# A fourth pair of token tiles in the seven-product scheme of the v stage, and six products of later pairs made in the head

## The chip, the cores and the metric

The kernel runs on one core of a Trainium2 chip. The metric is the device time of one execution in microseconds; lower is better. A matmul runs on TensorE (PE), which accumulates into PSUM banks of 128x512 float32. ScalarE (ACT) and VectorE (DVE) move and combine data, GpSimd (POOL) issues the transfers that add into their destination, SyncE (SP) issues most of the others.

## The reference

One block on x of 1024 tokens by 1024 channels, all float32. Cut to what matters:

```python
h = rmsnorm(x, norm_g)
proj = h @ w_in                                   # 1024 x 7424
q, k, v, za, u, vs, zs, gm = split(proj)          # vs, u: 1024 columns each; k, v: 128 each
...                                               # attention branch a
sgo = chunked_spatial_gating(gelu(u), gelu(vs), sg_w, sg_b, sg_ln_g, sg_ln_b)
sgo = (sgo * silu(zs)) @ w_sg_out
ga, gs = split(sigmoid(gm + b_merge))
x = x + (ga * a + gs * sgo) @ w_o
out = rmsnorm(x, final_g)
```

`chunked_spatial_gating` applies a layernorm to gelu(vs) along the channels and mixes it within blocks of 128 positions, so gelu(vs) is needed with the tokens on partitions. Every other projection is made with its output channels on partitions.

## The kernel before

**Products.** A float32 operand is split into a high part (rounded to the matmul's format, a cast on ACT) and a low part (the rest, a subtraction on DVE); a product of two such operands takes three matmuls: high by high, high by low, low by high. A block product is 128 output rows by 512 columns over 512 of k: four steps of k by three, 12 matmuls, in one PSUM bank.

**The seven-product scheme.** A pair of 128-row tiles of one operand against 1024 columns over 1024 of k would be eight block products. The kernel makes seven, with sums and differences of the quarters of the other operand. Those forms are called b11, t1, t2, b21, t3, b22 and t4 (`FORMS`); each is held as a high and a low array of 128x4x512 (`new_b`). In the stages after the head the normalized input is the side with forms, made once, and the weights come in pairs of tiles ("pairs", `gemm_pair`), numbered n = 0, 1, ...: four of u (n = 0 to 3), one of key and value (4), four of q (5 to 8), and so on. Pair n takes seven parts of its weights: parts 0 and 1 are the two halves of the first raw tile, 2 to 5 come from two tiles of sums, 6 is half of the second raw tile. Products run in the order b11 (part 0), t1 (2), t2 (3), b21 (1), t3 (4), b22 (5), t4 (6). `split_next` makes the high and low arrays of the next parts in tiles `wh` and `wl`, of which there are three each; `pair_job` loads the raw tiles (`wr`, three in all) and `sums` makes the two tiles `s`.

**The head (the v stage).** The eight token tiles of x are loaded (`load_x`, into `wr`), scaled, transposed on TensorE (`scaled_part`) and moved out of PSUM into the float32 quarters f11, f21 (tiles 0 to 3) and f12, f22 (tiles 4 to 7); `cast_part` makes b11, b21 and b22 from the same banks. Here the tokens are the stationary side, and token tile p is paired with tile p + 4. `vs_gemm(t)` multiplies tile t by the first 512 columns of the vs weights: 8 steps of k, 24 matmuls; for tiles 1 to 3 in two banks of four steps, one to go on being accumulated into by the scheme. Before the change the pairs are (1, 5), (2, 6) and (3, 7). Tiles 0 and 4 are done in full: tile 0 in `first_tiles`, tile 4 by `vs_gemm(4)`, and the second 512 columns of both by `plain(c)`, c = 0 to 3. `take(name, c)` makes half of a form's products (two of the four steps of k) for every pair; the five forms are t1, t2, t3, b22 and t4. Weights of the forms are sums of chunks of the vs weights: `chain` (two tiles `s`) and `apart`, into which POOL adds chunk after chunk (`add_to`), and `ask`, a raw tile with or without one addition.

**Order.** Where the code stands under `tc.manual_schedule`, PE, ACT and DVE run in the order in which it is written; elsewhere a planner orders each engine's work by its own estimates of cost, and it always orders SP and POOL. `after` adds an order between two instructions, `paced` makes a transfer wait for a given instruction; `part_of_early` issues one of the transfers that sum later weights in DRAM (`sums`), paced by matmuls.

**After the head** come the statistics of tiles whose gelu is complete, `normalize`, and `mix`, issued from `hook` inside the u pairs.

Of the kernel before, what the change touches and what calls it, by code (L numbers as in the profile page):

```python
# [25 lines left out]
F32 = mybir.dt.float32  # L26
# [6 lines left out]
P = 128  # L33
D = 1024
# [20 lines left out]
def hybrid_tile(  # L55
# [92 lines left out]
    y_dr = scratch("y_dr")  # L148

# [152 lines left out]

    def make_sums(first=None, most=2):

        for _ in range(min(most, len(sums_to_make))):
            sums_to_make.pop(0)(first)

    def pair_job(n, load):


        def job():
# [109 lines left out]
    def gemm_pair(b, finish, hook=lambda: None, second="o", begun=None, last_form=None):  # L421
# [24 lines left out]
        t2 = bank(second)[:]  # L446
        product(t2, ready[n, 1], b["b21"], True)
# [185 lines left out]
    b12 = [mtile([P, 4, P], F32R, "x", 5)[:] for _ in range(2)]  # L633
# [54 lines left out]
    def normed_tile(t, scale=None):  # L688
        xt, r = scale or scale_of(t)
        if t == 4:  # L690
            hb.update(new_b(("b22",)))
            f.update((n, slot(at, dt=F32)) for n, at in (("f12", "t4h"), ("f22", "t3h")))
        for j in range(2):
            p3, copy, _, _ = scaled_part(t, j, xt, r)
            if t <= 4 or j:
                cast_part(t, j, p3)
            nc.scalar.copy(*copy)
# [34 lines left out]
    def vs_gemm(t, middle=None):  # L732

        acc = vs_acc[t] = bank("o" if t in (2, 3) else "mm")[:]
# [4 lines left out]
        for k in range(KC):  # L739
            if middle and k in middle:  # L740
                middle[k]()
            if t < 4 and k == 4:
                nc.scalar.copy(dst, acc)
                part = vs_acc["p1"]
            pace[0] = vs_step(part, t, k, *vs_w[k], (0, KC - 1) if t == 4 else (k & 4, k | 3))
        if t == 4:
            nc.scalar.copy(dst, acc)
        else:
            nc.vector.tensor_add(dst, dst, part)
# [13 lines left out]
    def first_tiles():  # L763
# [24 lines left out]
        acc0 = bank("mm")  # L788
        n_first = [0]

        def first_steps(k, *kinds):
            hi, lo = (v[:, k % 4, :] for v in quarter_of(0, k // 4))
            wh, wl = vs_w[k]
            for kind in kinds:
                lt, rt = {"hh": (hi, wh), "lh": (lo, wh), "hl": (hi, wl)}[kind]
                mm = nc.tensor.matmul(acc0[:], lt, rt, start=n_first[0] == 0, stop=n_first[0] == 3 * KC - 1)
                n_first[0] += 1
# [31 lines left out]
        nc.scalar.copy(xh[:, 0, 0:HALF], acc0[:])  # L829
# [31 lines left out]

    first_tiles()
    marks = []
    for t in range(5):
        if t == 4:
            vs_gemm(t, {2: lambda: marks.append(pace[0])})
        elif t > 1:
            vs_gemm(t)
        if t + 3 < NT:
            normed_tile(t + 3)  # L870
        if t == 3:
            x_in[7] = load_x(7)
        if t == 2:
            for c in range(2):
                chain.append(mtile([P, D], F32, "s", 2))
                copy_to(chain[c][:], w[W_VS + 4 + c])
        if t == 3:
            for c in range(2):
                of_chain(c)
            ask(6)  # L880
        if t == 4:
            for c in range(2):
                paced(add_to(chain[c][:], w[W_VS + 6 + c]), marks[0])
            copy_to(apart[:], w[W_VS + 4])
            add_to(apart[:], w[W_VS + 6])
            add_to(apart[:], w[W_VS])
            ask(7)
            of_raw()
# [5 lines left out]
    BY_SUMS = (0, 4, 5, 6, 7)  # L894
# [32 lines left out]
    t5s = {1: bank("tp")[:], 2: bank("tp")[:], 3: vs_acc[4]}  # L927

    def plain(c):
        wh, wl = weights[c]  # L930
        for t in (0, 4):
            for k in range(2):
                pace[0] = vs_step(others[t], t, 2 * c + k, wh[:, half_of(k)], wl[:, half_of(k)])
            if c == 3:
                gelu_of(t, 1, others[t])
# [3 lines left out]
    def take(name, c, done=None):  # L939
# [39 lines left out]
    others = {t: bank("sc")[:] for t in (0, 4)}  # L979
    def first_form(t):  # L980
        part = f11[:, :, tokens(t)]
        nc.vector.tensor_sub(part, part, f12[:, :, tokens(t)])

    for t in (4, 5, 6):
        first_form(t)
    with tc.manual_schedule(engines={mybir.EngineType.PE, mybir.EngineType.Activation, mybir.EngineType.DVE}):
        hb.update(new_b(("t1",)))
        first_form(7)
        form("t1", f11, (0,))
        plain(0)  # L990
        of_raw()
# [9 lines left out]
        for c in range(2):  # L1001
            ask(c, 4 + c)
# [153 lines left out]
    late.extend(lambda t=t: statistics_of(t) for t in (1, 2, 3))  # L1156
# [1191 lines left out]
```

## Time and profile before

| | |
|---|---|
| median of 3 runs | 894.8 us (894.44 to 895.01) |
| the profiled execution | 893.94 us |
| its span in the trace | 892.1 us |
| PE busy | 883.2 us, 4143 matmuls |
| DVE, ACT, POOL busy | 702.0, 560.5, 164.1 us |
| mean DMA rate | 239 GB/s |
| first matmul of form t1 of the v stage | 55.7 us |
| first matmul of u pair 0 | 96.5 us |

The page of the profile gives the busy time of each engine and the chain of work that ended last, followed back from the last instruction. Its groups and the answers of the trace name an instruction by line, engine, operation and output<-inputs (buffer numbers left out). Times are from the start of the span. Matmuls are pipelined, so a matmul that lasts 0.39 us in a row may start 0.23 us after the one before it; what counts is start to start.

### The profile page before, as it was taken

How to read it: one execution, taken by the hardware profiler on the slowest of the kernel's cores; microseconds unless marked ns; L12 is line 12 of the kernel's file. 1: busy time of each engine (PE TensorE's matmuls, PEld its weight loads, DVE VectorE, ACT ScalarE, POOL GpSimd, SP SyncE). 2: the span in 40 equal slices, each digit the busy share in tenths (PEclk: the TensorE clock that was granted, in tenths of full speed). 3: DMA queues.
4: the chain of work that ended last, by engine and by line, in shares of the span. 5: the costliest groups of instructions: out<-in, count | busy, mean ns of one | idle time of the engine just before them, and what ended most of it. 6: DMA issues, size and time to landing. Idle time of an engine off the chain costs nothing.

```text
span 892.1 us, 13277 instructions
## 1 busy us (share of the span) xinstructions
PE 883.2 (99%) x4143; PEld 732.8 (82%) x4143; DVE 702.0 (79%) x1358; ACT 560.5 (63%) x1096; POOL 164.1 (18%) x267
## 2 busy tenths in 40 slices
PE   8999999999999999999999999999999999999997
PEld 5888888888888888888888888888888888888886
DVE  7978866676688779888889887665798699579986
ACT  7877833333444568889888896443575385467444
POOL 3112122214021012323222100122201111110013
PEclk9999999999999999999999999999999999999999
DMA  8687588879788889999999993889869557988533
GB/s 291 162 216 191 171 167 177 179 208 265 256 269 266 277 238 247 285 302 283 284 343 291 280 258 116 302 318 251 228 190 345 198 198 262 293 253 274 193 112 125
DMA packets 131541, 213.32 MB, mean 239 GB/s; under 512 B 13100, under 2 KB 60848, under 8 KB 131472
## 3 DMA queue, kind: packets, MB, share of 16 engines
q1 hardware_dynamic: 108648, 148.83, 51.2%
q0 software_dynamic: 22672, 63.45, 30.1%
q8 instruction: 33, 0.54, 0.3%
q14 instruction: 36, 0.29, 0.1%
q10 hardware_dynamic: 152, 0.20, 0.1%
HBM read 155.68 MB, written 90.31 MB: 276 GB/s over the span
## 4 chain that ended last, share of the span: by engine, by line
PE 98%; DMA 1%; DVE 0%; SPq 0%; issue 0%; DVEq 0%; ACT 0%; ACTq 0%
PE ps_mm L399 45%; PE ps_o L399 27%; PE ps_tp L399 4%; PE ps_mm L701 2%; PE ps_two L1502 2%; PE ps_o L701 2%; PE ps_sc L399 2%; PE ps_sc L701 2%; PE ps_tp L1132 2%; PE ps_o L1639 2%; PE ps_tp L1577 2%; PE ps_tp L701 1%; PE ps_o L1647 1%; DMA wr<-in_x_dram 1%; PE ps_tp L1589 1%; PE ps_tp L678 1%
## 5 line engine op out<-in xcount | busy, mean ns | idle before, releaser
L189 DVE TENSOR_TENSOR wl<-wr,wh 128x512 fp32r<-128x512 f32 (+1 forms) x65 | 61.7, 951 | 71.6 <-ACT wh L188 71.4
L188 ACT CAST wh<-s 128x1024 fp32r<-128x1024 f32 (+1 forms) x68 | 67.8, 1000 | 73.4 <-issue 22.1
L188 ACT CAST wh<-wr 128x512 fp32r<-128x512 f32 (+1 forms) x65 | 54.0, 832 | 65.2 <-PE ps_mm L399 35.4
L189 DVE TENSOR_TENSOR wl<-s,wh 128x1024 fp32r<-128x1024 f32 (+1 forms) x68 | 79.2, 1164 | 8.8 <-ACT wh L188 8.4
L351 POOL DMA_DIRECT2D sums<-in_w_dram x48 | 35.3, 742 | 183.9 <-PE ps_mm L399 86.9
L399 PE MATMUL ps_o<-T_t1h,wh 128*128 128x512 f32 x148 | 58.4, 395 | 0.0
L399 PE MATMUL ps_o<-T_b22h,wh 128*128 128x512 f32 x148 | 57.9, 391 | 0.0
L399 PE MATMUL ps_o<-T_t1h,wl 128*128 128x512 f32 x148 | 57.8, 391 | 0.0
L399 PE MATMUL ps_o<-T_b22h,wl 128*128 128x512 f32 x148 | 57.8, 390 | 0.0
L399 PE MATMUL ps_o<-T_b22l,wh 128*128 128x512 f32 x148 | 57.8, 390 | 0.0
L399 PE MATMUL ps_o<-T_t1l,wh 128*128 128x512 f32 x148 | 57.7, 390 | 0.0
L1549 ACT ACTIVATE pr<-pr,sm 128x193 f32<-128x193 f32 (+2 forms) x128 | 56.0, 440 | 1.7 <-DVE sm L1533 1.0
L399 PE MATMUL ps_mm<-T_t4h,wh 128*128 128x512 f32 (+1 forms) x144 | 56.4, 392 | 0.0
L399 PE MATMUL ps_mm<-T_t3h,wh 128*128 128x512 f32 x140 | 55.5, 396 | 0.0
L399 PE MATMUL ps_mm<-T_t4h,wl 128*128 128x512 f32 (+1 forms) x144 | 55.4, 385 | 0.0
L399 PE MATMUL ps_mm<-T_t4l,wh 128*128 128x512 f32 (+1 forms) x144 | 55.4, 385 | 0.0
L399 PE MATMUL ps_mm<-T_b11h,wh 128*128 128x512 f32 x140 | 54.8, 392 | 0.0
L399 PE MATMUL ps_mm<-T_t3h,wl 128*128 128x512 f32 x140 | 54.7, 391 | 0.0
L399 PE MATMUL ps_mm<-T_b11l,wh 128*128 128x512 f32 x140 | 54.7, 390 | 0.0
L399 PE MATMUL ps_mm<-T_t3l,wh 128*128 128x512 f32 x140 | 54.6, 390 | 0.0
L399 PE MATMUL ps_mm<-T_b11h,wl 128*128 128x512 f32 x140 | 54.6, 390 | 0.0
L399 PE MATMUL ps_mm<-T_t2h,wl 128*128 128x512 f32 x140 | 54.6, 390 | 0.0
(500 smaller groups left out, 2531.8 us busy)
## 6 DMA issues: line engine op xcount, KB each, us to landing
wr<-in_w_dram SPq DMA_DIRECT2D x80, 256.0 KB
sums<-in_w_dram POOLq DMA_DIRECT2D x24, 512.0 KB, 6.6
s<-sums SPq DMA_DIRECT2D x24, 512.0 KB
wr<-in_w_dram SPq DMA_DIRECT2D x17, 512.0 KB
q_hl<-qhl SPq DMA_DIRECT2D x16, 512.0 KB
q<-q_hl SPq DMA_DIRECT2D x64, 128.0 KB
y_dr<-x POOLq DMA_DIRECT2D x28, 256.0 KB, 6.5
s_dr<-x SPq DMA_DIRECT2D x24, 256.0 KB
```

The source lines that it names most:

```text
L188: hi_casts.append(nc.scalar.copy(hi, src))
L189: return nc.vector.tensor_sub(lo, src, hi.bitcast(F32))
L351: return lambda: paced(nc.gpsimd.dma_start(dst, src, accum_op=op))
L399: mm = nc.tensor.matmul(acc, lt, rt, start=fresh and k == 0 and n == 0, stop=k == 3 and n == 2, skip_group_check=True,)
L678: turn = nc.tensor.transpose(pt[:, i * P : (i + 1) * P], xt[:, k * P : (k + 1) * P], ident[:])
L701: mm = nc.tensor.matmul(acc, lt, rt, start=first and n == 0, stop=last and n == 2, skip_group_check=True)
L1132: nc.tensor.matmul(pm[:, t * P : (t + 1) * P], xh[:, half * 4 + t, g * P : (g + 1) * P], bias[-1][1][:, g % 2, :], start=True, stop=True,)
L1502: nc.tensor.matmul(st.sc[:, i], q_of[:, c, i * P : (i + 1) * P], kt[:, :, lo:hi], start=True, stop=True)
L1549: nc.scalar.activation(v, v, AF.Exp, bias=st.nmax[:, c, i : i + 1], scale=-1.0, accum_out=st.sums[:, c, i : i + 1])
L1577: nc.tensor.transpose(st.inner[0 : P if st.t else 64, at : at + P], st.pr[:, i, place_of(c, 64 if st.t else P, 192)], ident[:],)
L1589: nc.tensor.transpose(st.ends[0:wide, i * P : (i + 1) * P], st.pr[:, i, 129 : 129 + wide], ident[:])
L1639: nc.tensor.matmul(st.po[:], lt, rt, start=i == 0, stop=False, skip_group_check=True)
```

## The change

Pair (0, 4) joins the scheme: `take` runs over p = 2, 3, 0, 1, tile 0 keeps its two halves of k in two banks, and `plain` and `vs_gemm(4)` go. Between the transposes of tiles 4 to 7 and form t1 stand instead six block products: the b21 product of pairs n = 0 to 5, whose form b21 is complete once tile 3 is transposed. Their weights (part 1 of each pair) are loaded into the unused second half of `xh` (`ask_ahead`), split in twos (`ahead_weights`), multiplied (`make_ahead`), copied by ACT and stored in DRAM (`copy_ahead`, tile `made_dr`). In `gemm_pair` pairs 0 to 5 read that product back: `split_next` splits only part 0 and loads the made product into the other half of the `wh` tile, and the x11 addition takes it from there in place of a PSUM bank. The transposes of tiles 4 to 7, the product of tile 3 and the six products stand in an order written out by hand. The chain additions of chunks 6 and 7 are issued with the chain's copies, no longer paced. Cut to its core:

```diff
+    made_dr = scratch("made_dr", (6, P, HALF))
...   # split_next
+        n = keys[0][0]
+        if keys == [(n, 0)] and n in IN_HEAD:
+            ready[n, 1] = hi[:, HALF:D].bitcast(F32)
+            copy_to(ready[n, 1], made_dr[n])
...
+    IN_HEAD = range(6)
...   # pair_job
+            first = (r0[:, 0:HALF], [(n, 0)]) if n in IN_HEAD else (r0[:], [(n, 0), (n, 1)])
...   # gemm_pair
-        t2 = bank(second)[:]
-        product(t2, ready[n, 1], b["b21"], True)
+        if n in IN_HEAD:
+            t2 = ready[n, 1]
+        else:
+            t2 = bank(second)[:]
+            product(t2, ready[n, 1], b["b21"], True)
         term[0] = nc.vector.tensor_add(x11[:], x11[:], t2)
...   # the head
+    def ask_ahead(n):
+        loads_of[n](xh[:, n, HALF:D], 0, 1)
+
+    def ahead_weights():
+        n = 2 * len(split_ahead)
+        parts = []
+        for tag in ("wh", "wl"):
+            parts.append(mtile([P, D], F32R, tag, 3))
+        split(*(v[:].rearrange("p (c n) -> p c n", c=2) for v in parts), xh[:, n : n + 2, HALF:D])
+        split_ahead.append(parts)
+
+    def make_ahead():
+        n = len(to_copy)
+        acc = vs_acc["p0" if n % 2 == 0 else "p1"]
+        product(acc, [v[:, half_of(n % 2)] for v in split_ahead[n // 2]], hb["b21"], True)
+        to_copy.append(acc)
+
+    def copy_ahead(n):
+        v = xtile()
+        pace[0] = nc.scalar.copy(v[:], to_copy[n])
+        copy_to(made_dr[n], v[:])
...
+    x_in[3] = load_x(3)
+    for n in (0, 1):
+        ask_ahead(n)
+    x_in[4] = load_x(4)
+    for n in range(2, 6):
+        ask_ahead(n)
+    normed_tile(3)
...
+    vs_gemm(2)
+    ahead_weights()
+    for c in range(2):
+        chain.append(mtile([P, D], F32, "s", 2))
+        copy_to(chain[c][:], w[W_VS + 4 + c])
+        add_to(chain[c][:], w[W_VS + 6 + c])
+    copy_to(apart[:], w[W_VS + 4])
+    add_to(apart[:], w[W_VS + 6])
+    add_to(apart[:], w[W_VS])
...
+    with ORDERED:
...
+        scale_both(4)
+        scales[5] = scale_of(5)
+        add_third = vs_gemm(3, {4: lambda: turn(4)}, True)
+        move_out(4)
+        scale_both(5)
+        ahead_weights()
+        scales[6] = scale_of(6)
+        add_third()
+        x_in[7] = load_x(7)
+        make_ahead()
+        turn(5)
+        scale_both(6)
+        scales[7] = scale_of(7)
+        make_ahead()
+        ask(0, 4)
+        copy_ahead(0)
+        move_out(5)
+        turn(6)
+        scale_both(7)
+        first_form(4)
+        ahead_weights()
+        make_ahead()
+        move_out(6)
+        copy_ahead(1)
+        ask(1, 5)
+        turn(7)
+        first_form(5)
+        first_form(6)
+        make_ahead()
+        move_out(7)
+        copy_ahead(2)
+        first_form(7)
...   # take
-        for p in (1, 2, 3):
+        for p in (2, 3, 0, 1):
...   # the five forms
         form("t1", f11, (0,))
-        plain(0)
-        of_raw()
+        of_chain(0)
+        make_ahead()
+        copy_ahead(3)
         form("t1", f11, (1,))
-        plain(1)
-        of_chain(0)
-        gelu_of(0, 0)
-        plain(2)
         of_chain(1, 1)
-        gelu_of(1, 0, n=3)
-        gelu_of(4, 0)
-        plain(3)
+        make_ahead()
+        copy_ahead(4)
+        copy_ahead(5)
+        for t in (0, 2):
+            gelu_of(t, 0, n=2)
```

`turn(t)` is the eight transposes of a tile, `scale_both(t)` its two scalings on DVE, `move_out(t)` its three moves on ACT and one low part on DVE, `first_form(t)` the subtraction f11 - f12 for its tokens.

More of the change, by code (lines that the diff above doesn't have):

```diff
@@ L308, in pair_job @@
     def pair_job(n, load):
+        loads_of.append(load)
         def job():
@@ L730, in hybrid_tile, with vs_gemm @@
     vs_acc = {}
-    def vs_gemm(t, middle=None):
-        acc = vs_acc[t] = bank("o" if t in (2, 3) else "mm")[:]
+    def vs_gemm(t, middle=None, later=False):
+        acc = vs_acc[t] = bank("sc" if t == 1 else "o")[:]
         part = acc
@@ L741, in vs_gemm @@
                 middle[k]()
-            if t < 4 and k == 4:
+            if k == 4:
                 nc.scalar.copy(dst, acc)
                 part = vs_acc["p1"]
[L745 to L749, printed above, removed]
+            pace[0] = vs_step(part, t, k, *vs_w[k], (k & 4, k | 3))
+        add = lambda: nc.vector.tensor_add(dst, dst, part)
+        return add if later else add()
     def in_order(*steps):
@@ L786, in first_tiles @@
         act = in_order(act, wide)
-        acc0 = bank("mm")
-        n_first = [0]
+        halves = [bank("mm")[:] for _ in range(2)]
+        vs_acc[0], vs_acc["p0"] = halves
+        n_first = [0, 0]
         def first_steps(k, *kinds):
@@ L795, in first_steps @@
                 lt, rt = {"hh": (hi, wh), "lh": (lo, wh), "hl": (hi, wl)}[kind]
-                mm = nc.tensor.matmul(acc0[:], lt, rt, start=n_first[0] == 0, stop=n_first[0] == 3 * KC - 1)
-                n_first[0] += 1
+                e = k // 4
+                mm = nc.tensor.matmul(
+                    halves[e], lt, rt, start=n_first[e] == 0, stop=n_first[e] == 11, skip_group_check=True
+                )
+                n_first[e] += 1
                 after(mm, turns[-1])
@@ L828, in first_tiles @@
         vs_gemm(1, {4: lambda: both(3, "hl"), 5: lambda: normed_tile(2, third)})
-        nc.scalar.copy(xh[:, 0, 0:HALF], acc0[:])
+        nc.scalar.copy(xh[:, 0, 0:HALF], halves[0])
+        nc.vector.tensor_add(xh[:, 0, 0:HALF], xh[:, 0, 0:HALF], halves[1])
         for move in (kept[1], kept[2], copy):
@@ L860, in of_raw @@
         weights.append(vs_weights(waiting.pop(0)[:]))
-    first_tiles()
[L863 to L887, printed above, removed]
-            of_raw()
+    def ask_ahead(n):
+        loads_of[n](xh[:, n, HALF:D], 0, 1)
@@ new lines, in copy_ahead, with first_form @@
+    def copy_ahead(n):
+        v = xtile()
+        pace[0] = nc.scalar.copy(v[:], to_copy[n])
+        copy_to(made_dr[n], v[:])
+    def first_form(t):
+        part = f["f11"][:, :, tokens(t)]
+        nc.vector.tensor_sub(part, part, f["f12"][:, :, tokens(t)])
+    first_tiles()
+    x_in[3] = load_x(3)
[5 more added lines that the diff above has]
+    normed_tile(3)
+    for t in (5, 6):
+        x_in[t] = load_x(t)
@@ new lines, in hybrid_tile, with scale_both @@
+    vs_gemm(2)
[7 more added lines that the diff above has]
+    add_to(apart[:], w[W_VS])
+    scales = {4: scale_of(4)}
+    ORDERED = tc.manual_schedule(
+        engines={mybir.EngineType.PE, mybir.EngineType.Activation, mybir.EngineType.DVE}
+    )
+    parts = {}
+    def scale_both(t):
+        xt, r = scales[t]
+        for j in range(2):
+            cs = half_of(j)
+            nc.vector.scalar_tensor_tensor(
+                xt[:, cs], xt[:, cs], r[:], g_sb[:, cs], op0=ALU.mult, op1=ALU.mult
+            )
@@ new lines, in turn, with move_out @@
+    def turn(t):
+        xt, _ = scales[t]
+        parts[t] = []
+        for j in range(2):
+            pt = bank("tp")
+            for i in range(4):
+                k = j * 4 + i
+                nc.tensor.transpose(pt[:, i * P : (i + 1) * P], xt[:, k * P : (k + 1) * P], ident[:])
+            parts[t].append(pt[:].rearrange("p (k c) -> p k c", k=4))
+    def move_out(t):
+        one, two = parts[t]
+        nc.scalar.copy(f["f12"][:, :, tokens(t)], one)
+        cast_part(t, 1, two)
+        nc.scalar.copy(f["f22"][:, :, tokens(t)], two)
@@ new lines, in hybrid_tile @@
+    with ORDERED:
+        hb.update(new_b(("b22",)))
+        f.update((n, slot(at, dt=F32)) for n, at in (("f12", "t4h"), ("f22", "t3h")))
+        scale_both(4)
[30 more added lines that the diff above has]
+        first_form(7)
@@ L925, in form @@
             split(hi[:, cs, :], lo[:, cs, :], src[:, cs, :], name == "t2")
[L927 to L935, printed above, removed]
+    t5s = {0: vs_acc["p0"], 1: vs_acc["p1"], 2: bank("tp")[:], 3: bank("tp")[:]}
     NAMES = ("t1", "t2", "t3", "b22", "t4")
@@ L942, in take @@
         into = t5s if name in ("t1", "b22") else vs_acc
-        wh, wl = weights[4 + 2 * s + c]
+        wh, wl = weights[2 * s + c]
         hi, lo = hb[name]
-        for p in (1, 2, 3):
+        for p in (2, 3, 0, 1):
             for k in range(2):
@@ L1045, in hybrid_tile @@
         make_sums()
-        variance_of(4)
         take("b22", 1, both_terms)
         split_next()
-        means_of(5, 3)
-        for t in (1, 2, 3):
+        means_of(4, 4)
+        for t in range(4):
             statistics(t, 0)
@@ L1057, in hybrid_tile @@
         variance_of(t)
-    for t in (0, 4):
-        nc.vector.tensor_scalar_mul(mv[:, t, 1:2], mv[:, t, 1:2], 1.0 / D)
-    nc.vector.tensor_scalar_mul(mv[:, 5:8, 1], mv[:, 5:8, 1], 1.0 / D)
+    nc.vector.tensor_scalar_mul(mv[:, 4:8, 1], mv[:, 4:8, 1], 1.0 / D)
     split_next()
@@ L1155, in hybrid_tile @@
     by_products[0] = True
-    late.extend(lambda t=t: statistics_of(t) for t in (1, 2, 3))
+    late.extend(lambda t=t: statistics_of(t) for t in range(4))
     late.append(normalize)
```

26 lines of the change are left out of this document (7 added, 19 removed).

## The prediction

> **What bounds the kernel now.** I read the page first: the shares of the engines and the chain of work that ended last.
>
> ```profile
> span 892.1 us, 13277 instructions
> PE 883.2 (99%) x4143; PEld 732.8 (82%) x4143; DVE 702.0 (79%) x1358; ACT 560.5 (63%) x1096; POOL 164.1 (18%) x267
> PE 98%; DMA 1%; DVE 0%; SPq 0%; issue 0%; DVEq 0%; ACT 0%; ACTq 0%
> ```
>
> TensorE is the chain. A busy share of 99% could still hide stretched work, so the second view is the list of waits of TensorE in the first 125 us, which cover all the work that is edited by hand:
>
> ```profile
> PE ps_o L611 <- DVE T_b22l L117: 1.5, 1, 1.5
> PE ps_mm L796 <- ACT T_t2h L720: 0.7, 1, 0.7
> PE ps_tp L678 <- DVE wr L673: 0.5, 1, 0.5
> ```
>
> Columns: total wait, times, longest. All three lie in the first 13 us, which keep their form. The third view is busy time by stretch: tiles 2 to 4 and the plain products; the five forms of the v stage; the first u pair; u pairs 1 to 3. Columns: width, then PE, PEld, DVE, ACT and POOL busy, granted clock, DMA share, GB/s.
>
> ```profile
> 20.00:55.70 35.70, 35.64 (x181) 29.10 (x180) 28.56 (x55) 28.65 (x51) 4.70 (x6) 1.00 0.75 201
> 55.70:96.50 40.80, 40.80 (x182) 33.79 (x181) 35.16 (x51) 30.73 (x53) 7.90 (x14) 1.00 0.77 186
> 96.50:118.50 22.00, 22.00 (x111) 18.68 (x110) 20.93 (x41) 15.04 (x22) 2.02 (x3) 1.00 0.49 143
> 118.50:188.30 69.80, 69.80 (x363) 59.55 (x362) 45.22 (x69) 24.40 (x36) 16.08 (x22) 1.00 0.88 194
> ```
>
> TensorE has no hole in the stages that change, at a clock of 1.00. So the edit is worth what it takes off TensorE, minus any hole that it opens. In the chain of waits one block product of twelve 128x512 matmuls (four of k, three of high and low parts) stands as
>
> ```profile
> 99.36 2.72 PE ps_o L399 x12
> ```
>
> that is, 0.227 us for each matmul.
>
> **The sum on TensorE.** Removed from the head: tile 4's first half (24 matmuls, its own product loop) and the four plain chunks (4 x 2 tiles x 2 x 3 = 48), 72 in all. Put in their place: six products of 12, again 72. Added in the five forms: a fourth pair, 5 x 2 chunks x 2 x 3 = 60. Removed later: the b21 product of pairs 0 to 5 (four u, key-value, first q), 6 x 12 = 72. Net: -72 + 72 + 60 - 72 = -12 matmuls, 12 x 0.227 = **-2.72 us**. The head should last 60 x 0.227 = 13.6 us longer and the six pairs 16.3 us shorter.
>
> The second term is the transposes. Before, tiles 4 and 5 are turned in two groups of four, broken by matmuls; tile 7 in one group of eight:
>
> ```profile
> 29.80 0.39 PE L701 MATMUL ps_o<-T_t1h,T_b11h 128*128 128x512 f32 x1
> ...
> 31.16 0.39 PE L701 MATMUL ps_o<-T_t1h,T_b11h 128*128 128x512 f32 x1
> 31.61 0.63 PE L678 MATMUL ps_tp<-ident,wr 128*128 128x128 f32 x4
> ...
> 32.98 0.40 PE L701 MATMUL ps_o<-T_t1h,T_b11h 128*128 128x512 f32 x1
> ...
> 43.68 0.39 PE L701 MATMUL ps_mm<-T_t2h,T_b22l 128*128 128x512 f32 x1
> 43.91 1.03 PE L678 MATMUL ps_tp<-ident,wr 128*128 128x128 f32 x8
> ...
> 45.02 0.40 PE L701 MATMUL ps_sc<-wl,T_b11h 128*128 128x512 f32 x1
> ```
>
> From 31.16 to 32.98 are 1.82 us with three matmuls started (0.68) and eight transposes: 1.14 for the eight. From 43.68 to 45.02 are 1.34 with two matmuls (0.45): 0.89. The changed block turns tiles 4 to 7 eight at a time, so I take 0.25 from tile 4 and some of it from tile 5: **-0.4 us** (bounds 0 and -0.75, three tiles).
>
> **Edits costed at nothing, and what covers them.** The new block fixes the order on PE, ACT and DVE, so I laid it out with these groups of 20 to 60 us (busy, mean ns):
>
> ```profile
> L667 ACT ACTIVATE wl<-wr 128x1024 f32<-128x1024 f32 x4 | 4.3, 1069 | 0.0
> L667 ACT ACTIVATION_READ_ACCUMULATOR wl<-wr 128x1 f32 x4 | 0.8, 197 | 0.0
> L188 ACT CAST wh<-s 128x1024 fp32r<-128x1024 f32 x4 | 4.2, 1044 | 0.0
> L684 ACT CAST T_b22h<-ps_tp 128x512 fp32r<-128x512 f32 x4 | 2.4, 597 | 0.0
> L159 ACT ACTIVATE st<-st,eps_sb 128x1 f32<-128x1 f32 x5 | 1.5, 308 | 0.0
> L673 DVE SCALAR_TENSOR_TENSOR wr<-wr,st,g_sb 128x512 f32<-128x512 f32 x12 | 8.4, 745 | 0.0
> L982 DVE TENSOR_TENSOR T_t3l<-T_t3l,T_t4h 128x512 f32<-128x512 f32 x4 | 2.7, 683 | 0.8 <-ACT T_t4h L697 0.8
> ```
>
> Tile 2's product ends as before, at 29.8, where the first row above starts tile 3's. TensorE then: half of tile 3's product to 32.5, turn 4 to 33.4, the other half to 36.1, made product 0 to 38.8, turn 5 to 39.7, made 1 to 42.4, turn 6, made 2, turn 7 to about 47, made 3, 4 and 5 to 55.2, then form t1: half a microsecond ahead of the 55.7 of before. ACT: three moves of tile 4 (3 x 0.6) to 35.2, the cast of the weights of products 2 and 3 (1.0) to 36.2, square and root of tile 6 (1.1 + 0.2 + 0.3) to 37.8, the same of tile 7 to 39.4, copy of product 0 to 40.0, three moves of tile 5 to 41.8. The bank for turn 6 must be free at 42.4: slack 0.6, the smallest that I find. On DVE the add that ends tile 3 stands behind tile 6's statistics, at about 39, and made product 1 needs its bank at 39.7. From turn 7 (47) ACT has three moves, copy 2, a form cast, a weight cast and copy 3, 1.8 + 0.6 + 1.0 + 1.0 + 0.6 = 5.0, to 52.0; made 5 needs that bank at 52.4. So the block closes with margins of half a microsecond.
>
> What queues behind the waits: tile 7's square on ACT holds the copy of product 0 and the moves of tile 5, and through them turn 6; on SP its load can go out only after turn 4 (33.4), behind the second-half loads and the chain loads, which wait for nothing. It must land by 38.4, that is within 5.0. Before:
>
> ```profile
> 18.00 15.31 SPq L591 DMA_DIRECT2D wr<-in_x_dram  x4
> 37.16 1.07 ACT L667 ACTIVATE wl<-wr 128x1024 f32<-128x1024 f32 x1
> 39.38 1.75 POOL L237 DMA_DIRECT2D s<-in_w_dram  x2 [13.51 <-DVE wr L673]
> sums<-in_w_dram POOLq DMA_DIRECT2D x8, 512.0 KB, 5.2
> ```
>
> The last of the four loads went out at about 33.0 and was read at 37.16: at most 4.2 us. But the two chain additions went out at 39.4, behind a pace; now nothing holds them back, and they run beside the loads of tiles 4 to 7. The last row is a 512 KB addition into DRAM: 5.2 us from issue to landing. So the ends are 0 (4.2 against 5.0) and, for a load that takes twice the 5.2, a hole of 10.4 - 5.0 = 5.4 us; a gain is excluded, since TensorE had no hole there to fill. I take 0, because the 4.2 is the same load.
>
> By the Trainium skill, "DMA: Bandwidth & Descriptors", section "Anatomy of one DMA", a transfer takes 2.0 us and its bytes at 436 GB/s: for 512 KB an estimate of 3.2 us. Its section "Queues, rings and completion order" says that each DMA engine alternates between queues packet by packet, so beside POOL's additions the part that depends on size doubles: 4.4 us. No run here shows the landing itself; by either, the load is in time and the sum stays.
>
> **After the head.** Pairs 0 to 5 split half as much of their first raw tile, store nothing new, and load 256 KB of a made product each, behind the first cast of their pair and three products ahead of its use; the x11 addition reads SBUF in place of PSUM, the same 128x512. Two things are denser. In the first u pair DVE is at 20.93 of 22.00; minus 2.72 of width, plus 0.3 (one more tile of statistics, half a split less), it overflows by 1.9 us into pairs 1 to 3, where it is 65% busy. What would be late is the split of the first sum:
>
> ```profile
> 115.75 1.23 DVE L189 TENSOR_TENSOR wl<-s,wh 128x1024 fp32r<-128x1024 f32 x1
> 122.38 0.39 PE L399 MATMUL ps_o<-T_t1h,wh 128*128 128x512 f32 x1
> ```
>
> Ready at 117.0, used at 122.4: 5.4 us of slack, less 2.7 and 1.9, leaves 0.8. I take 0, bounds 0 and +2. DMA is the other: pairs 1 to 3 keep 0.88 x 69.8 = 61.4 us of it, in 61.6 us, with 0.75 MB of made products more.
>
> Sum: -2.72 - 0.4 + 0 = **-3.1 us**. The profiled execution took 893.94 around its span of 892.1; 890.8 would follow for it. The median of the runs is 894.8, 0.9 above, so I predict **891.7 us** for the median, -0.35%.
>
> **Rivals.** (a) *A hole in the hand-ordered block takes the gain.* For it: margins of 0.5 us at four places, and ACT's queue behind one load. Against: that load took under 4.2 us, and TensorE waited nowhere in 13 to 125 us before. A hole of 1.3 to 5.4 us gives 893.0 to 897.1, most likely about 894. By the Trainium skill, "TensorE: Matmul & The Clock Gate", Part 1, an idle window of about 3.4 us halves the clock; the longest wait here is 1.5 us, and the granted clock is 1.00 throughout, so no run shows that; only the upper half of (a) would come to it.
>
> (b) *DVE in the first u pair becomes the bound*: the 1.9 us of overflow lands on the normalization or on the first sums. For it: 20.93 of 22.00. Against: 0.8 us of slack remains. Price up to 2 us: 892.5 to 893.7.
>
> (c) *Slower: DMA bounds u pairs 1 to 3.* Its share goes from 0.88 to 1.00 or over. One mechanism: the second raw tile of pair 2 is late, then its sums, then form t1.
>
> ```profile
> 129.18 0.81 SPq L240 DMA_DIRECT2D wr<-in_w_dram  x2
> 137.30 0.68 DVE L294 TENSOR_TENSOR s<-wr 128x512 f32<-128x512 f32 x1
> 140.98 1.23 DVE L189 TENSOR_TENSOR wl<-s,wh 128x1024 fp32r<-128x1024 f32 x1 [0.46 <-ACT wh L188]
> 145.12 0.39 PE L399 MATMUL ps_o<-T_t1h,wh 128*128 128x512 f32 x1
> ```
>
> Now: 7.3 us from issue (130.0) to use, then 2.9 us from the split (142.2) to form t1. It decides when such a load takes over 10.2 us, twice the 5.2 us of the 512 KB addition. If DMA then holds those three pairs at their old length, 3 x 2.72 = 8.2 us are lost: 899.9.
>
> (d) *The change gives no fewer matmuls in effect*, because the filling of before was hidden: excluded, TensorE has no idle time there.
>
> **How the numbers follow.** Forecast 62% (its own range 890.4 to 893.0: three tiles of transposes, and small waits under 1.3). (a) 19%: of it 4 faster, 11 same, 4 slower. (b) 9%: 3, 5, 1. (c) 10%: 1 same, 9 slower. About 0.2%, 1.8 us, is what these runs tell from no change. Faster 0.62 - 0.02 (small waits) + 0.04 + 0.03 = 0.67; same 0.02 + 0.11 + 0.05 + 0.01 = 0.19; slower 0.14. The range of 8 in 10 goes from 890.3 (the sum's low end, 3.5 off the profiled execution's 893.94, is 890.4) up through (a) and (b) to 896.0, the first part of (c), which leaves about 1 in 10 above and little below.
>
> **What would show it.** Right: 12 fewer matmuls of 128x512; form t1 starting near 55; the five forms lasting 54.4 us (20 products of 2.72) in place of 40.8; the last form ending near 110; u pairs about 2.7 us shorter; no new line in TensorE's waits. Wrong: a TensorE wait for ACT or DVE between 33 and 55 (a), between the last form and the end of the first pair (b), or for wl or s in pairs 1 to 3 with a DMA share of 1.0 (c); or transposes that cost 1.1 a tile as before (the -0.4).

## The result, and the profile after

| | before | after |
|---|---|---|
| median | 894.86 us (7 runs, 894.44 to 895.92) | 903.82 us (898.87 to 905.29) |
| profiled execution, span | 893.94, 892.1 us | 903.82, 901.9 us |
| matmuls | 4143 | 4131 |
| waits of TensorE after 40 us | none over 0.3 us | 2.5 and 4.7 us, 0.3, 0.2 |

The changed kernel is slower: the ratio is 1.0079, interval 1.0053 to 1.0105. The forecast was 891.7, range 890.3 to 896.0. (Medians count every execution, ranges and ratios leave out disturbed ones, here one of 5091 us: without it the median after is 902.0, and the six left lie at 898.9 to 900.2 and, the profiled one among them, at 903.8 to 905.3.) The twelve matmuls are gone, as counted; the span is 9.7 us longer all the same. Lines have moved: the product of a pair, L399 before, is L410; the split is L189 (ACT) and L190 (DVE), the sums L296 to L300, the move of x22 L451, the x11 addition L462, y22 L469.

The list of waits of TensorE in the changed kernel (total, times, longest):

```profile
PE ps_o L410 <- ACT x L451: 7.1, 2, 4.7
PE ps_o L625 <- DVE T_b22l L117: 1.5, 1, 1.5
PE ps_tp L689 <- DVE wr L684: 1.1, 1, 1.1
PE ps_tp L947 <- ACT T_t3h L954: 0.3, 1, 0.3
```

The second and third belong to the first 13 us. The fourth is the predicted weak point at turn 6. The first is new: two holes, neither in the head nor in the u pairs. Busy time by stretch, cut at the first matmul of each pair, says where. First pairs 3, 4 (key and value) and 5 (first q) of before, then the same three after (width, PE, PEld, DVE, ACT, POOL busy, clock, DMA share, GB/s):

```profile
164.44:188.31 23.87, 23.87 (x128) 20.39 (x126) 15.24 (x24) 8.45 (x12) 4.56 (x7) 1.00 0.88 236
188.31:208.05 19.74, 19.74 (x92) 16.16 (x90) 12.42 (x19) 6.78 (x11) 4.75 (x7) 1.00 0.73 178
208.05:227.65 19.60, 19.60 (x90) 16.08 (x88) 12.28 (x19) 8.48 (x12) 6.62 (x10) 1.00 0.93 274
```

```profile
171.94:192.42 20.48, 20.48 (x109) 17.41 (x108) 14.44 (x25) 6.47 (x10) 4.56 (x7) 1.00 0.95 250
192.42:212.22 19.80, 17.34 (x80) 13.84 (x78) 11.46 (x19) 6.15 (x11) 6.45 (x9) 1.00 0.91 225
212.22:233.34 21.12, 16.44 (x65) 12.99 (x64) 8.60 (x13) 5.96 (x10) 4.82 (x8) 0.84 0.71 224
```

Pair 3 is 3.4 us shorter without a hole. Pairs 4 and 5 have 12 matmuls fewer each and are no shorter: PE is busy for 17.3 of 19.8 and for 16.4 of 21.1 us, and in pair 5 the granted clock falls to 0.84. (The row of pair 5 is even too short: one matmul of pair 6, at 233.34, runs ahead of the twelve of pair 5's form t4, which fall outside the row.) The chain of waits, followed back from TensorE's start at 225.79, gives the way (start, length, what):

```profile
210.76 0.65 SPq L241
211.46 8.78 DMA wr<-in_w_dram
...
220.36 0.06 DVE s L299
...
220.97 1.22 DVE wl L190
...
223.31 0.69 DVE vt L190
223.99 0.61 DVE x L462
224.63 0.04 ACT wh L189
...
225.15 0.60 ACT x L451
...
225.79 3.36 PE ps_o L410 x7
```

Read upward from the end: TensorE's form b22 adds into the bank that x22's move must first read, and waits for that move; the move stands on ACT behind a cast whose `wh` tile still holds the made product; the x11 addition that frees it stands on DVE behind the sums of pair 6; the sums wait for the last quarter of pair 6's second raw tile, 8.78 us after its issue. The same wait of DVE is in the trace of before, and there it hit nobody. Before, then after, pairs 4 and 5 of each:

```profile
194.23 0.69 DVE L294 TENSOR_TENSOR s<-wr 128x512 f32<-128x512 f32 x1 [2.97 <-DMA wr<-in_w_dram]
211.34 0.84 DVE L294 TENSOR_TENSOR s<-wr 128x512 f32<-128x512 f32 x1 [3.06 <-DMA wr<-in_w_dram]
```

```profile
199.72 0.69 DVE L299 TENSOR_TENSOR s<-wr 128x512 f32<-128x512 f32 x1 [4.16 <-DMA wr<-in_w_dram]
220.36 0.69 DVE L299 TENSOR_TENSOR s<-wr 128x512 f32<-128x512 f32 x1 [7.75 <-DMA wr<-in_w_dram]
```

Counted from the first matmul of pair 5, in which it is read, the second tile of pair 6 is there 3.3 us in before (211.34 - 208.05) and 8.1 us in after (220.36 - 212.22). TensorE also asks sooner for what hangs on it. In before, form b22 of pair 5 stands behind b21 and t3, 14.2 us in. After, the planner puts its first matmuls right behind t2, so that it is due 8.7 us in. The first row is the start of b22 in before, the second the end of t2 after:

```profile
222.21 0.39 PE L399 MATMUL ps_o<-T_b22h,wh 128*128 128x512 f32 x1
```

```profile
220.73 0.39 PE L410 MATMUL ps_mm<-T_t2h,wl 128*128 128x512 f32 x1
```

From the starts of the matmuls, the 9.7 us of span come from: +0.3 in the first 23 us, which are the same work; +0.3 up to form t1 (predicted -0.4); +13.6 in the five forms; -10.1 in pairs 0 to 3 (predicted -10.9); +4.3 in pairs 4 and 5 up to the t1 product of pair 6 (predicted -5.4); +0.5 in all that follows, and +0.8 after TensorE's last matmul (7.0 us in place of 6.2). So 9.7 of the 12.8 us between the sum and the span were lost in two pairs: 7.1 in the holes and most of the rest in the slow clock behind the second.

### The profile page after: what moved, and what is told of

It is laid out like the page before. It is cut to its first block, busy times and chain, and to the rows that moved or that the text cites. A ratio compares the mean times of both kernels' runs of the same rounds, so it can differ in the third digit from the quotient of the medians.

```text
span 901.9 us, 13264 instructions
## 1 busy us (share of the span) xinstructions
PE 884.4 (98%) x4131; PEld 732.4 (81%) x4131; DVE 698.9 (77%) x1354; ACT 559.2 (62%) x1097; POOL 164.0 (18%) x267
## 4 chain that ended last, share of the span: by engine, by line
PE 91%; DMA 4%; DVE 2%; ACT 1%; SPq 1%; issue 1%; DVEq 0%; ACTq 0%
PE ps_mm L410 43%; PE ps_o L410 24%; PE ps_tp L410 4%; PE ps_sc L410 3%; PE ps_sc L712 2%; DMA wr<-in_w_dram 2%; PE ps_o L712 2%; PE ps_two L1580 2%; PE ps_tp L1655 2%; PE ps_o L1717 2%; PE ps_mm L712 2%; DMA wr<-in_x_dram 1%; PE ps_tp L1210 1%; PE ps_tp L712 1%; PE ps_o L1725 1%; PE ps_tp L1667 1%
## 5 line engine op out<-in xcount | busy, mean ns | idle before, releaser
L189 ACT CAST wh<-s 128x1024 fp32r<-128x1024 f32 (+1 forms) x66 | 65.9, 1001 | 75.6 <-PE ps_mm L410 21.8
L190 DVE TENSOR_TENSOR wl<-wr,wh 128x512 fp32r<-128x512 f32 (+1 forms) x63 | 56.1, 892 | 61.9 <-ACT wh L189 59.3
L189 ACT CAST wh<-wr 128x512 fp32r<-128x512 f32 (+1 forms) x63 | 49.3, 783 | 68.0 <-PE ps_mm L410 32.4
L190 DVE TENSOR_TENSOR wl<-s,wh 128x1024 fp32r<-128x1024 f32 (+1 forms) x66 | 76.4, 1158 | 9.3 <-ACT wh L189 8.7
L410 PE MATMUL ps_o<-T_b22h,wh 128*128 128x512 f32 x148 | 59.1, 399 | 7.1 <-ACT x L451 7.1
L410 PE MATMUL ps_o<-T_t1h,wh 128*128 128x512 f32 x148 | 58.5, 395 | 0.0
L410 PE MATMUL ps_o<-T_b22h,wl 128*128 128x512 f32 x148 | 58.2, 394 | 0.0
L410 PE MATMUL ps_o<-T_b22l,wh 128*128 128x512 f32 x148 | 58.1, 393 | 0.0
L410 PE MATMUL ps_o<-T_t1h,wl 128*128 128x512 f32 x148 | 57.8, 391 | 0.0
L410 PE MATMUL ps_o<-T_t1l,wh 128*128 128x512 f32 x148 | 57.7, 390 | 0.0
L410 PE MATMUL ps_mm<-T_t4h,wh 128*128 128x512 f32 (+1 forms) x144 | 56.3, 391 | 0.0
L410 PE MATMUL ps_mm<-T_t3h,wh 128*128 128x512 f32 x140 | 55.9, 399 | 0.0
L410 PE MATMUL ps_mm<-T_t4h,wl 128*128 128x512 f32 (+1 forms) x144 | 55.4, 385 | 0.0
L410 PE MATMUL ps_mm<-T_t4l,wh 128*128 128x512 f32 (+1 forms) x144 | 55.4, 385 | 0.0
L410 PE MATMUL ps_mm<-T_b11h,wh 128*128 128x512 f32 x140 | 55.0, 393 | 0.0
L410 PE MATMUL ps_mm<-T_t3l,wh 128*128 128x512 f32 x140 | 54.9, 392 | 0.0
L410 PE MATMUL ps_mm<-T_t3h,wl 128*128 128x512 f32 x140 | 54.9, 392 | 0.0
L410 PE MATMUL ps_mm<-T_t2h,wh 128*128 128x512 f32 x140 | 54.6, 390 | 0.0
L410 PE MATMUL ps_mm<-T_b11l,wh 128*128 128x512 f32 x140 | 54.6, 390 | 0.0
L410 PE MATMUL ps_mm<-T_b11h,wl 128*128 128x512 f32 x140 | 54.6, 390 | 0.0
```

Source lines behind the costliest of these rows:

```text
L189: hi_casts.append(nc.scalar.copy(hi, src))
L190: return nc.vector.tensor_sub(lo, src, hi.bitcast(F32))
L410: mm = nc.tensor.matmul(acc, lt, rt, start=fresh and k == 0 and n == 0, stop=k == 3 and n == 2, skip_group_check=True,)
```

## Experiments

All are edits of the changed kernel unless they say otherwise; ratios are to the kernel before on the same chip.

**Four runs on the way from DMA to TensorE.** First, the made product in the free half of the `wl` tile:

```diff
-            ready[n, 1] = hi[:, HALF:D].bitcast(F32)
+            ready[n, 1] = lo[:, HALF:D].bitcast(F32)
```

> The made product of pairs 0 to 5 is loaded into the unused half of the low tile (wl) in place of the high tile (wh); nothing else differs. The low tile's slot is taken next by a subtraction on DVE, the engine that reads the made product, so no cast on ACT waits any more for the x11 addition. Theory S (the slot: late raw tile -> DVE sums -> x11 addition behind them -> ACT cast of part 6 into its slot -> ACT move of x22 behind it -> TensorE form b22): the waits of TensorE on ACT's x22 move (7.1 us in two) fall to under 1 us and the low clock after them goes, although DVE still waits about 12 us for the raw tiles; 891 to 894 us. Theory D (the transfers are too dense, and whatever waits for the late raw tile ends in TensorE): TensorE waits 5 us or more in pairs 4 and 5 in another place; 898 to 903 us.

906.24 us, 1.0124 (1.0110 to 1.0137). Waits of TensorE:

```profile
PE ps_mm L410 <- DVE x L469: 4.3, 1, 4.3
PE ps_o L410 <- ACT x L451: 2.2, 1, 2.2
PE ps_o L410 <- DVE wl L190: 1.7, 1, 1.7
```

The `wh` slot alone is not the cause: with it freed, 8.2 us of holes come out in place of 7.1, of which 2.2 are still at x22's move and the rest at y22 and at a low part. Next, the sums of pairs 5 and 6 behind the x11 addition:

```diff
         term[0] = nc.vector.tensor_add(x11[:], x11[:], t2)
+        if n in (4, 5):
+            behind_of[n + 1] = term[0]
```

> The made product stays in the high tile; for pairs 4 and 5 the sums of the next pair are ordered behind the x11 addition on DVE. Theory S: the addition no longer stands behind the wait for the raw tile, the slot comes free in time, the waits of 7.1 us go; 891 to 894 us. Theory D: no change beyond 2 us; 898 to 903 us.

902.69 us, 1.0082 (1.0067 to 1.0097). Pair 4 lost its hole (17.2 us long). Pair 5 kept 3.0 and 2.4 us, because there the made product itself is late, on the same DMA engines, and the raw tile again stands before y22:

```profile
218.74 0.69 DVE L462 TENSOR_TENSOR x<-x,wh 128x512 f32<-128x512 f32 x1 [6.42 <-DMA wh<-made_dr]
224.70 0.69 DVE L299 TENSOR_TENSOR s<-wr 128x512 f32<-128x512 f32 x1 [5.28 <-DMA wr<-in_w_dram]
```

Then four products in the head (pairs 4 and 5 make their own again), and none:

```diff
-    IN_HEAD = range(6)
+    IN_HEAD = range(4)      # the other run: range(0), and no ahead pieces
```

> Only the four u pairs get a made product; pairs 4 (key-value) and 5 (first q) make their own b21 product as before, and the head makes four products. The count of matmuls is that of the change. Theory S: pairs 4 and 5 are as before, the u pairs keep their gain; the head may wait 0.5 to 1 us before form t1, with less to fill; 891.5 to 894 us. Theory D, if the dense stretch of the u pairs is what makes the later loads late: waits of 2 us or more stay in pairs 4 and 5; 896 to 900 us.

> The seven-product scheme for the fourth pair alone: no product is made ahead, all pairs make their own b21. Shows what the filling covers in the head. Both theories: no wait in pairs 4 and 5. TensorE's work between tile 3's product and form t1 is 3 us of transposes, while the chain of tiles 5 to 7 through ACT and DVE and the form takes about 14: a hole of 9 to 13 us in the head, part of it at a low clock after it; 899 to 906 us.

Four: 898.07 us, 1.0030 (1.0019 to 1.0041); its profiled execution, 895.61, is its fastest; the other five take 897.8 to 898.7, and no profile shows where. In the profiled one pairs 4 and 5 take 39.35 us together (39.34 before) without a wait, though pairs 0 to 3 are short and the DMA share in pair 3 is 0.99. The head now shows what the products fill: TensorE waits 2.7 us there. None: 906.36 us in one execution, with 10.6 us of waits in the head. So with this traffic the loss needs pairs 4 and 5 to be short.

**What makes the raw tile late.** The keys stored once (each later load of keys in two halves); the products of the head given to other pairs; the made loads of pairs 4 and 5 left out; and, in the kernel before, 2 MB of stores more:

```diff
-            for dup in range(2):
+            for dup in range(1):        # stores of k_dr, here and in rotate_keys
...   # the second run
-    IN_HEAD = range(6)
+    IN_HEAD = (0, 1, 2, 3, 9, 10)
...   # the third, n in (4, 5)
+                ready[n, 1] = hi[:, 0:HALF].bitcast(F32)
...   # the fourth, in the kernel before
+                for to in (k_dr, k_more):
```

> The changed kernel, but the keys are stored into DRAM once and not twice: four of the eight 256 KB stores of the key-value pair go (1 MB), and each later load of keys reads the one copy in two transfers. Theory B (burst): the raw tile of the next pair lands 8 us or more after its issue because the stores of keys and values (2 MB and 1.5 MB) fill the DMA engines in just the two pairs that were shortened. With 1 MB less the second raw tile of pair 6 lands 2 to 4 us earlier; the holes of 2.5 and 4.7 us in pairs 4 and 5 shrink to under 3 us in all, the clock stays near 1.00 between 215 and 240 us, time 893 to 898. Theory M (made load): the 256 KB read of the made product stands ahead of the raw tile on SP's queue and is what delays it; the stores do not matter; holes as before, 902 to 905. Theory L (latency): such a load in 512-byte pieces takes 8 us whatever runs beside it; 902 to 905.

903.0 us, 1.009 (1.007 to 1.011). The tile of pair 6 is read at 214.87, 1.4 us into pair 5 and not 8.1: the stores were what delayed it. The time did not follow. The hole of pair 4 (2.6 us) stands before the first store of keys, as it must; a hole of 2.2 came in pair 5, where ACT now waits for a store of the values (`DMA v_dr<-vt`, 4.77 us). One of 2.1 us came in the attention, before a load of q. Whether the doubled reads of keys cause it is not shown: the two runs with deferred additions, below, have one of 2.0 and 2.5 us before the same load.

> The changed kernel, but the six products made in the head belong to pairs 0 to 3, 9 and 10 (the first two of zs) in place of 0 to 5: the key-value pair and the first q pair make their own b21 product again and are as long as in the kernel before. Same number of matmuls as the changed kernel. If the loss sits in pairs 4 and 5 alone (theories B, M and L): no hole there, pairs 9 and 10 shorter by 2.7 us each, time 891.5 to 895. Rival (any shortened pair that follows one with a loaded weight tile stalls): new holes of 2 to 5 us at pairs 9 and 10, time 897 to 905.

894.71 us, 0.9996 (0.9980 to 1.0012). Pairs 4 and 5 are clean, 19.7 and 19.6 us. At 288.7 this run stands 3.0 us behind before, as it should with two pairs to come; pairs 9 and 10 and the start of the attention then give 2.9 of the 5.4 us, with holes of 0.65 (ACT's move of x22) and 0.85 us.

> The changed kernel, but pairs 4 and 5 do not load their made products: the x11 addition takes the high part of their part 0 in its place, so both pairs are as short as in the changed kernel, the wh slot is held as long, and only the two 256 KB loads are gone (the made product is left out of the result of these two pairs). Theory M: holes of pairs 4 and 5 gone, 891 to 895. Theories B and L: the raw tile of pair 6 still lands some 7 us after its issue, holes of 4 to 7 us remain in all, 898 to 904.

900.82 us, 1.0062 (1.0045 to 1.0079); 6.4 us of holes remain, and the tile of pair 6 comes 7.7 us into pair 5. Without the made loads the holes are 0.7 us smaller; they have a share and are not the cause.

> The kernel before, with the eight 256 KB stores of keys made a second time, into a scratch array that nobody reads (2 MB more DMA traffic in the key-value pair). Theory B: the raw tile of pair 6 lands 4 to 8 us later than its 211.3 us and TensorE gets a hole in pair 5, as in the changed kernel although no pair is shortened: time 899 to 908. Theories M and L: the load is not later, at most the POOL queue is longer: 894 to 896.

906.33 us, 1.0142 (1.0101 to 1.0183), no pair shortened. Pair 6's tile moved from 211.34 to 218.09:

```profile
218.09 0.69 DVE L295 TENSOR_TENSOR s<-wr 128x512 f32<-128x512 f32 x1 [8.40 <-DMA wr<-in_w_dram]
238.29 0.69 DVE L295 TENSOR_TENSOR s<-wr 128x512 f32<-128x512 f32 x1 [10.05 <-DMA wr<-in_w_dram]
```

The lateness (+6.75 us) is as expected, the place is not. Pair 5, full length, took it without a hole; the hole of 4.5 us is one pair later, where the next tile was late in turn. Three of 0.8 to 1.6 us follow.

**Moving traffic.** The six products for pairs 0 to 3, 6 and 7; POOL's additions of pairs 3 and 4 put into pairs 6 and 7; the same with the x11 order of above; and the additions moved forward into the five forms and u pair 0:

```diff
-    IN_HEAD = range(6)
+    IN_HEAD = (0, 1, 2, 3, 6, 7)
...   # the second run, with part_of_early(1) in the hooks of pairs 6 and 7
-        part_of_early(1 if 1 < done[0] <= KC // 2 else 2)
+        if done[0] not in (4, 5):
+            part_of_early(1 if 1 < done[0] <= KC // 2 else 2)
...   # the last run
-            if s > 1 and p == 1:
+            if s > 1 and p in (1, 3):
...
+        if done[0] not in (4, 5):
+            part_of_early(1)
```

> The changed kernel, but the six products of the head belong to pairs 0 to 3, 6 and 7 (second and third q pair), which run from 230 to 270 us, where the DMA share is 0.67 to 0.76 and POOL adds little. Theory B (a short pair stalls where the DMA engines are already full): no hole at 200 and 221, pairs 6 and 7 shorter by 2.7 us each without a new hole, so 2 to 2.7 us under the run with pairs 9 and 10, and 891.5 to 893.5. Rival R (a pair without its own b21 product stalls wherever weights come in 512-byte pieces, since the sums stand at the head of VectorE's queue): holes of 2 to 5 us in pairs 6 and 7, 896 to 904.

896.29 us, 1.0011 (0.9995 to 1.0026). Pairs 6 and 7 took 17.6 and 16.5 us in place of 20.0 and 19.0, as the theory has it; pairs 8 and 10 behind them gave 2 us back (20.2 and 20.0 us in place of 19.0 and 19.2, with holes of 0.7 and 0.5), which it had not, so the time is over its 891.5 to 893.5.

> The changed kernel, but POOL's early additions that pairs 3 and 4 issue (some ten of 256 to 512 KB) come in pairs 6 and 7 instead. Theory B: the second raw tile of pair 5 lands about 5.5 us after its last issue in place of 7.2, the hole at 200 us goes (2.5 to under 0.5 us); at pair 6 the stores of keys and values stay, so of the 4.7 us at 221 some 1 to 4 remain; 896 to 902. Theory L (latency of 512-byte pieces alone): both holes as before, 902 to 905.

914.51 us, 1.022 (1.0189 to 1.0250). Busy time in pairs 4, 5 and 7 of this run:

```profile
191.50:208.70 17.20, 17.20 (x80) 13.84 (x79) 11.45 (x19) 6.26 (x11) 3.89 (x6) 1.00 0.66 191
208.70:225.80 17.10, 17.10 (x78) 13.78 (x77) 11.59 (x18) 8.21 (x13) 4.06 (x6) 1.00 0.89 275
245.70:271.60 25.90, 20.94 (x85) 16.84 (x84) 14.99 (x25) 8.26 (x12) 8.04 (x12) 0.93 0.98 291
```

Both holes are gone, with the stores, the made loads and the order on DVE untouched: more than I expected. They came back, larger, where the additions went: holes of 5.0 and 6.4 us in pairs 7 and 8, the first, by the chain of waits, behind a store of q (`DMA q_hl<-qhl`) of 11.6 us. The time missed both forecasts.

> As the run with deferred additions, and the sums of pairs 5 and 6 stand behind the x11 addition on VectorE. Theory B: the two together leave under 1.5 us of holes in pairs 4 and 5; 893 to 898. Theory L: as the run with x11 first alone, one hole of 3 to 5 us, 901 to 904.

913.99 us, 1.0216 (1.0188 to 1.0245): the same holes at the same places, so the order on DVE has nothing left to add once the traffic is gone.

> The changed kernel, with POOL's early additions moved out of pairs 3 and 4 the other way: into the five forms and u pair 0, where the DMA share is 0.54 to 0.59 (a second addition in each of the last three forms' chunks, every hook in place of every second in pair 0, none in pairs 3 and 4). Theory B (DMA traffic is conserved: it stalls TensorE wherever it meets a full stretch and costs nothing where there is room): no holes over 0.5 us at 200 and 221 and none where the additions went; the arithmetic of the change then shows at last: head +14.2, u pairs -10.1, pairs 4 and 5 -5.4, the tail +0.5 to +1.4, so a span of 891.5 to 893 and a time of 892 to 895. Rival (the additions now stand ahead of the chain of vs weights on POOL's queue, or of the raw tiles of pairs 1 and 2): new TensorE waits in the forms or in pairs 1 and 2, 896 or more.

894.01 us, 0.9992 (0.9983 to 1.0001). Busy time from pair 0 to pair 5, and all the waits of TensorE:

```profile
110.00:131.68 21.68, 21.65 (x114) 18.32 (x112) 19.11 (x39) 16.16 (x26) 7.18 (x8) 1.00 0.98 181
...
172.46:192.94 20.48, 20.48 (x109) 17.40 (x108) 14.45 (x25) 6.45 (x10) 0.00 (x0) 1.00 0.53 138
192.94:210.14 17.20, 17.20 (x80) 13.84 (x78) 11.43 (x19) 6.26 (x11) 3.89 (x6) 1.00 0.64 190
210.14:227.22 17.08, 17.08 (x78) 13.75 (x76) 11.47 (x18) 8.21 (x12) 4.87 (x8) 1.00 0.92 276
```

```profile
PE ps_o L625 <- DVE T_b22l L117: 1.5, 1, 1.5
PE ps_mm L807 <- ACT T_t2h L731: 0.9, 1, 0.9
PE ps_tp L947 <- ACT T_t3h L954: 0.4, 1, 0.4
PE ps_tp L689 <- DVE wr L684: 0.2, 1, 0.2
```

u pair 0 takes a DMA share of 0.98 without a hole, pairs 4 and 5 are 17.2 and 17.1 us long, and the ratio comes back from 1.0079 to 0.9992, some 8 us. It is the best of the versions; whether it beats the kernel before, by 0.1%, is just inside the measurement's doubt.

**Held slot or short pair.** Pairs 4 and 5 without made load and without hold (the x11 addition adds x11 to itself, the made product of both is left out); and the loads kept, into a tile of their own:

```diff
-            t2 = ready[n, 1]
+            t2 = x11[:] if n in (4, 5) else ready[n, 1]
...   # the second run
+            ready[n, 1] = xtile()[:] if n in (4, 5) else hi[:, HALF:D].bitcast(F32)
```

> The run without the made loads, and the wh slot is not held either: in pairs 4 and 5 the x11 addition adds x11 to itself (the made product of these two pairs is left out of the result), so both pairs are short but nothing waits for a slot until the addition is done. The raw tile of pair 6 should again land 6 to 8 us after its last issue. Theory H (the hold is what turns the late load into a hole): ScalarE's cast of part 6 no longer stands behind the x11 addition, holes of pairs 4 and 5 under 1 us in all, 890 to 894. Theory B2 (a short pair cannot take such a landing, held slot or not, because VectorE's own later work, y22 and the low parts, stands behind the sums): holes of 2 to 6 us in all remain, now by VectorE, 896 to 902.

> The changed kernel, but pairs 4 and 5 load their made product into a tile of the five that x11, x12 and x22 use, so that no wh or wl slot is held until the x11 addition is done; the loads stay. Theory H: hole in pair 4 under 0.5 us; in pair 5 a rest of 0 to 3 us, because the made load itself is late there; 892 to 897. Theory B2: holes of 4 to 7 us in all remain, 899 to 904.

901.86 us, 1.0073 (1.0053 to 1.0093), and 899.13 us, 1.0056 (1.0036 to 1.0075). The first:

```profile
PE ps_mm L411 <- DVE x L470: 3.9, 1, 3.9
PE ps_o L411 <- DVE wl L190: 2.6, 1, 2.6
...
PE ps_o L411 <- ACT x L452: 1.3, 1, 1.3
```

The hold made the hole of pair 4 about one us longer (2.5 against 1.3 and 1.6). Pair 5 still loses 6.4 and 5.4 us without it. So in these short pairs the late tile reaches TensorE by one way or another.

## Why the prediction was wrong

- **Twelve matmuls, -2.72 us: right.** 4143 to 4131. The forms last 54.4 us, as counted.
- **The transposes, -0.4: about right.** From tile 2's product (where before has 23.28) to form t1 it was 32.40 us; in ten of the other runs that keep the head's six products it is 32.0 to 32.2 us.
- **Rival (a), the load of tile 7: the mechanism is there, small.** I bounded it by the 4.2 us of the old load against 5.0. It took longer, ACT waited and turn 6 had a hole:

```profile
39.41 1.06 ACT L678 ACTIVATE wl<-wr 128x1024 f32<-128x1024 f32 x1 [1.09 <-DMA wr<-in_x_dram]
43.73 0.66 PE L947 MATMUL ps_tp<-ident,wr 128*128 128x128 f32 x4 [0.31 <-ACT T_t3h L954]
```

  It costs this execution and that of the version with early additions 0.6 to 0.7 us, those ten runs nothing. The chain of waits has 5.45 us for the load. By the Trainium skill, "DMA: Bandwidth & Descriptors", sections "Anatomy of one DMA" and "Queues, rings and completion order", my estimates were 3.2 alone and 4.4 beside a second queue; this trace is above both. The first of these sections gives its figures for transfers that GpSimd issues, and this load is issued by SP, so I had used them outside what the section states.
- **The u pairs: 0.8 to 0.9 us short of the 10.9**, in all runs with made products, without a wait. The 128 matmuls of the mixing take 13.9 us from start to start in place of 13.3; that is 0.6 of it.
- **Rivals (b) and (c): not there.** The first u pair has no hole. Pairs 1 to 3 keep 0.95 to 0.97 of DMA share and stall nowhere. But (c) had the way of the loss, a late second raw tile and then its sums; it had it in the wrong pairs.
- **The step that failed: "DMA is the other: pairs 1 to 3 keep 61.4 us of it in 61.6 us", and nothing said of pairs 4 and 5.** The idea was right, that shortened pairs leave the DMA engines the same bytes in less time, but I tested it on the stretch that I had in a table, to 188.3 us, and stopped where two of the six shortened pairs begin. There stand the transfers that the kernel writes in a burst, 2 MB of keys and 1.5 MB of values, beside raw tiles in pieces of 128 KB. The rows of before had it: DVE waiting 2.97 and 3.06 us for those tiles. Such a wait costs nothing as long as the work behind it has room; a pair 2.72 us shorter, with the traffic of all six packed into 16 us less, used the room up. Two things qualify this. The hole of pair 4 stands before the first store of keys, so POOL's additions, not the burst, go with it. And I took the order on TensorE as given, while b22 moved ahead of t3. The term that I set to 0 measured +7.1 us of holes and about 2.1 of slow clock in the profiled execution.
- **The clock.** I left it to the upper half of (a). It came in pair 5, behind the hole of 4.7 us: matmuls stand 0.43 us apart, not 0.227, for about ten of them.

```profile
225.79 0.80 PE L410 MATMUL ps_o<-T_b22h,wh 128*128 128x512 f32 x1 [4.68 <-ACT x L451]
226.39 0.63 PE L410 MATMUL ps_o<-T_b22l,wh 128*128 128x512 f32 x1
226.82 0.63 PE L410 MATMUL ps_o<-T_b22h,wl 128*128 128x512 f32 x1
```

  By the Trainium skill, "TensorE: Matmul & The Clock Gate", Part 1, an idle window of about 3.4 us halves the clock; for this hole the trace agrees.

**What is shown and what is not.** Shown: the loss is in pairs 4 and 5 (it goes when they are long again); it needs the traffic that makes the raw tile late (moving the additions away, forward or back, takes the holes out of both pairs; stores added to the kernel before make the tile late by 6.8 us and cost 11.7 us); neither the made loads nor the held slot explain it. Not shown: why pair 5 at full length took a tile 9.0 us into the pair, while the short ones did not take 7.7 to 10.5. The traces point at the order on TensorE. At full length b22 starts 14.2 us into pair 5 (at 223.24 in the run with more stores); in the short pairs 4 and 5 it is due 8.3 and 8.7 us in. That is 5.4 us sooner, half of it the missing product and half form t3, which the planner now puts behind. No run keeps t3 ahead of b22 in these short pairs, so how much of the holes hangs on that order is open; the order on DVE and ACT differs between them too. Also open is why, with the holes gone, the version with early additions gains some 0.5 us and not 3.1. Its profiled execution (span 892.4, 0.3 over before's) is 3.4 us off the sum: 0.7 in the first 23 us, 0.8 at the turns of the head, 0.8 in the u pairs, 0.4 in pairs 4 and 5, 0.8 after the last matmul, 0.1 the other way between; I tested none of them by itself.

## What to carry to other kernels

Work taken off a bound engine shortens every stretch for the DMA engines as well: make the table of DMA share for each shortened stretch, through the last one. Look in the trace of before for waits of an idle-looking engine on a transfer (here DVE, 3 us, twice); they are the slack that the change will spend, and what is queued behind them says who pays. Putting the waiting engine's work in another order mended one hole of the two; moving the traffic mended both: beside the best version, the same additions cost some 8 us where the change left them (ratio 1.0079 against 0.9992) and some 20 in pairs 6 and 7 (1.022); they cost no wait of TensorE where the share had been 0.54 to 0.59.

## What the hardware showed that I had not expected

The clock fell behind shorter holes too. Behind the first 30 us, fifteen traces (all but that with no product in the head, whose holes stand close together) have 33 holes over 0.6 us. All eleven of 3.0 us and more were followed by matmuls 0.43 us apart, none of eleven under 1.8 us was, and of eleven between 1.9 and 2.7 us seven were. That is below the 3.4 us of the page of the Trainium skill named above, and the measurement decides. Two from pair 4 of two runs, the made product in `wl` and the one without made loads:

```profile
202.75 0.80 PE L410 MATMUL ps_o<-T_b22h,wh 128*128 128x512 f32 x1 [2.24 <-ACT x L451]
203.34 0.63 PE L410 MATMUL ps_o<-T_b22l,wh 128*128 128x512 f32 x1
203.77 0.63 PE L410 MATMUL ps_o<-T_b22h,wl 128*128 128x512 f32 x1
```

```profile
202.66 0.50 PE L413 MATMUL ps_o<-T_b22h,wh 128*128 128x512 f32 x1 [2.14 <-ACT x L454]
202.99 0.40 PE L413 MATMUL ps_o<-T_b22l,wh 128*128 128x512 f32 x1
203.23 0.39 PE L413 MATMUL ps_o<-T_b22h,wl 128*128 128x512 f32 x1
```

And the issue itself can slow down. In the changed kernel the four pieces of the second raw tile took SP 2.5 us for pair 5 and twice as long for pair 6, which puts the last of them later before it has begun to wait. The DMA share does not tell the two apart: it is 1.07 in the first stretch and 1.03 in the second. With the keys stored once, the four pieces for pair 6 took 2.65 us at a share of 0.96. So for this tile the slow issue goes with the four key stores beside it; by what way is not shown.

```profile
190.00 2.52 SPq L241 DMA_DIRECT2D wr<-in_w_dram  x4
...
207.28 4.85 SPq L241 DMA_DIRECT2D wr<-in_w_dram  x4
```
